# A decoder block on one core: the output product of the next tokens moved in front of the last channel group of the feed-forward part, and GpSimd's tensor operations moved to VectorE

## The chip, the cores and the metric

The kernel runs on one core of a Trainium2 chip. A core has TensorE (PE, matrix products into PSUM), VectorE (DVE), ScalarE (ACT), GpSimd (POOL) and SyncE (SP), which here only issues transfers. Each engine works through its own queue in order. The metric is the device time of one execution in microseconds (us); lower is better. The kernel before took 2862.96 us (median of 3 runs, 2861.45 to 2866.43).

## The reference

One layer of a decoder for 2048 tokens of width 1024, in float32. In outline:

```
h = rmsnorm(x, norm1_g) * (1 + sc1) + sh1
p = h @ w_in                                   # 1024 -> 27 * 128 columns
y = concat(rglru(p...), hgrn2(p...), rwkv7(p...)) * mix_beta
x = x + g1 * (y @ w_out)                       # 1024 -> 1024
h = rmsnorm(x, norm2_g) * (1 + sc2) + sh2
x = x + g2 * ((silu(h @ w_gate) * (h @ w_up)) @ w_down)   # 1024 -> 2816 -> 1024
out = rmsnorm(x, final_g)
```

`sh1, sc1, g1, sh2, sc2, g2` come from the conditioning vector c by one product with `ada_w`. The three mixers are recurrences along the tokens: a gated linear recurrence behind a short convolution, a gated linear attention in chunks, and the delta-rule recurrence of RWKV-7.

## The kernel before

**Layout.** Channels lie on the 128 partitions, tokens along the free dimension. The 2048 tokens are cut into NB = 4 blocks of TB = 512; a tile is 128 channels by 512 tokens, and KC = 8 such tiles make up the width of 1024. D_FF = 2816 gives NF = 22 tiles of the feed-forward part.

**Products.** Every large product goes through `project` (L261). Operands are split in two: `hi`, rounded to the fast float32r format, and `lo`, what is left. A product of one 128x128 weight piece with one tile is three matmuls of 512 columns (`wh*hh`, `wh*hl`, `wl*hh`), L271. The results gather in PSUM banks named `pd`, of which there are 3. Weights come from `load_w` (L250): SyncE loads a tile `wr` (3 buffers), ScalarE makes `wh` and VectorE `wl` (4 buffers each), by `split_v`. The tiles of activations are `hh` and `hl`, 16 buffers each. Float32 tiles of the dense part (inputs, residuals, squares, intermediate results) are all of one name, `xs`, with 12 buffers.

**Order of work.** The program is written as one long list, and a planner sets each engine's queue from it when the kernel is built: it follows the dependencies, hands out the buffers of each name, and prefers the instruction with the smaller priority. The kernel sets the priority by `level(...)`: "out" (adds into the residual) comes first, then "load" (weights), "feed" (the default of the dense part), "mix" (mixers), and "dense" (the matmuls, and the final norm's multiplies) last. The mixers' steps are dealt out between the products by `tick` (L282), by a clock `now` that counts matmul time; `finish(b)` (L294) runs what is left of the mixers up to block b. So mixers overlap with `w_in` and with the feed-forward part of the earlier blocks.

**Stages.** `w_in_products` (L1001) stores the 27 column tiles of p to memory, for blocks 0 and 1, then 2 and 3 (L1111 to L1128); its last five columns run for block 2 and after that for block 3. Then, for each block b:

- `load_y(b)` (L1044): finishes the mixers of b, loads the eight tiles of y (`xs`), and splits them with `split` (L238): ScalarE for `hh`, GpSimd for `hl`.
- `w_out_products(b)` (L1054): for each of 8 channel tiles d the x tile is loaded (`xs`), the product is added to it (it becomes x1[d] and stays), and `square_sum` (L337) squares it into another `xs` tile and adds up. After the first channel it calls `before()`, which is the final norm of block b-1. At its end `rstd_of` (L354) sums over the partitions by matmuls with ones (L363 to L365) and takes Ln and Exp.
- `ffn(b)` (L1084): `make_h` (L388) writes the eight normalized tiles; `ffn_up` makes the 22 tiles g = silu(gate) * up; after each four of them the down products of that group (groups of 4, 4, 4, 4, 4, 2) are added into x1, for the eight channels d. Before the last group stands `load_y(b + 1)`. With the last group the squares for the final norm are taken.

The loop at its heart, with the last group as one of six:

```
for f0 in range(0, NF, 4):
    ...
    if len(gs) == NF and ys is None and b + 1 < NB:
        ys = load_y(b + 1)
    for d in range(KC):
        p, = project(gs[f0:f0 + n], load_w(w_down[d][:, f0 * 128:(f0 + n) * 128], split_v))
        with level("out"):
            stt(x1[d], p, G2[:, d:d + 1], x1[d], OP.mult, OP.add)
```

GpSimd does three things: the `lo` of `load_y` (L240), six additions in the statistics of block 1 (L344), and clearing of tiles (L609).

Of the kernel before, what the change touches and what calls it, by code (L numbers as in the profile page):

```python
# [10 lines left out]
F = mybir.dt.float32  # L11
# [63 lines left out]
def hybrid_kernel(ctx, tc, x, par, ada_w, w_in, rgw, igw, w_up, a_up, g_up, w_out,  # L75
# [14 lines left out]
    @contextmanager  # L90
    def level(name):

        clock[levels[-1]] = tc.cur_priority
        levels.append(name)
        tc.cur_priority = clock[name]
        yield
        clock[name] = tc.cur_priority
        levels.pop()
        tc.cur_priority = clock[levels[-1]]

    def act(o, i, f=AF.Copy, **k):
        return A.activation(o, i, f, **k)

    def stt(o, a, s, b, op0, op1):
        return V.scalar_tensor_tensor(o, a, s, b, op0=op0, op1=op1)
# [38 lines left out]
    def pc(name, i=0):  # L144
        a, b = PCOLS[name]
        assert a + i < b
        return P[:, a + i:a + i + 1]
# [87 lines left out]
                               lambda: bank("pd", 3), xs_)  # L235


    def split(src, hi, lo):  # L238
        act(hi, src)
        G.tensor_sub(lo, src, hi.bitcast(F))  # L240

    def split_v(src, hi, lo):
        i = act(hi, src)
        V.tensor_sub(lo, src, hi.bitcast(F))
        return i
# [4 lines left out]
    def load_w(src, fn):  # L250
        ws = []
        with level("load"):
            for c in range(0, src.shape[1], TB):
                n = min(TB, src.shape[1] - c)
                w = raw_w(src[:, c:c + n])
                hi, lo = w_parts()
                fn(w[:, :n], hi[:, :n], lo[:, :n])
                ws.append((hi, lo))
        return ws

    def project(h, *cols):  # L261

        ps = [bank("pd", 3) for ws in cols]
        tot = 3 * len(h)
        with level("dense"):
            for k, (hh, hl) in enumerate(h):
                c = slice((k % 4) * 128, (k % 4 + 1) * 128)
                for p, ws in zip(ps, cols):
                    wh, wl = ws[k // 4]
                    for n, (a, b) in enumerate(((wh, hh), (wh, hl), (wl, hh)), 3 * k):  # L270
                        PE.matmul(p, a[:, c], b, start=(n == 0), stop=(n == tot - 1))  # L271
                    now[0] += 0.68
                if k % (4 // len(ps)) == 4 // len(ps) - 1 or k == len(h) - 1:
                    tick()
        return ps
# [61 lines left out]
    def square_sum(s, t, k, tile=None, n=1):  # L337

        s, *last = s or (None,)
        if len(last) == n:  # L340
            if s is None:
                s = last.pop(0)
            else:
                (G if tile else V).tensor_add(s, s, last.pop(0))  # L344
        q = (tile or xs_)()
        if k == KC - 1:
            V.tensor_mul(q, t, t)
        else:
            squared[:] = [act(q, t, AF.Square)]
        return s, *last, q  # L350
# [18 lines left out]
    def load_x(src, b, k, tile=None):  # L369
        t = (tile or xs_)()  # L370
        load(t, src[k, :, b * TB:(b + 1) * TB])
        return t
# [15 lines left out]
    def make_h(xt, rs, gain, shift, table=None, ks=range(KC), over=True):  # L388

        hs = []  # L390

        def low(k, t, hi, lo):
            stt(lo, t, shift[:, k:k + 1], hi.bitcast(F), OP.add, OP.subtract)
            hs.append((hi, lo))

        todo = []
        for k in ks:
            x_ = xt(k)
            t = x_ if over else xs_()
            stt(t, x_, gain[:, k:k + 1], rs, OP.mult, OP.mult)  # L400
            hi, lo = parts_()
            i = act(hi, t, AF.Identity, bias=shift[:, k:k + 1])
            todo.append((k, t, hi, lo))
            if len(todo) > 2:
                low(*todo.pop(0))
        for a in todo:
            low(*a)
        if table is not None:
            order(A.preload_act_table_set(table), i)
        return hs  # L410

    def drain(it):
        for _ in it:
            pass
# [586 lines left out]
    def w_in_products(h, cols, side):  # L1001

        n = 0
        while n < len(cols):

            cs_ = cols[n:n + 2] if n == 0 and len(h) == 1 else cols[n:n + 1]
            ws = [W.pop(c) if c in W else load_w(w_in[c], split_v) for c in cs_]
            for i, b in enumerate(h):
                for j, (c, p) in enumerate(zip(cs_, project(h[b], *ws))):
                    with level("feed"):  # L1010
                        t = xs_()
                        if (n + i + j) % 2:
                            act(t, p)
                        else:
                            V.tensor_copy(t, p)
                        SP.dma_start(pd[c, :, b * TB:(b + 1) * TB], t)
                        stored.add((c, b))
                    next(side, None)
            n += len(cs_)
# [24 lines left out]
    def load_y(b):  # L1044
        finish(b)
        ys = []
        for k in range(KC):
            t = load_x(yd, b, k)
            y = parts_()
            split(t, *y)  # L1050
            ys.append(y)
        return ys

    def w_out_products(b, ys, before):  # L1054
        x1, s = [], None
        for d in range(KC):
            ws = load_w(w_out[d], split_v)
            t = load_x(x, b, d)
            p, = project(ys, ws)
            with level("out"):  # L1060
                stt(t, p, G1[:, d:d + 1], t, OP.mult, OP.add)
            if d == 0:
                before()
            s = square_sum(s, t, d)
            x1.append(t)
        return x1, rstd_of(s)

    def ffn_up(h, f):
        if f:
            p, = project(h, load_w(w_gate[f], split_v))  # L1070
        else:
            p, pu = project(h, load_w(w_gate[f], split_v), load_w(w_upf[f], split_v))
        t = xs_()
        with level("out"):
            act(t, p, AF.Silu)
        if f:
            pu, = project(h, load_w(w_upf[f], split_v))
        with level("out"):
            V.tensor_mul(t, pu, t)
        g = parts_()  # L1080
        split_v(t, *g)
        return g

    def ffn(b, x1, rs):  # L1084
        h = make_h(lambda k: x1[k], rs, A2, B2, "silu_and_others", over=False)
        gs, s, ys = [], None, None
        for f0 in range(0, NF, 4):
            n = min(4, NF - f0)
            while len(gs) < min(f0 + n + (2 if f0 + n + 2 >= NF else 1), NF):
                gs.append(ffn_up(h, len(gs)))  # L1090
            if len(gs) == NF and ys is None and b + 1 < NB:
                ys = load_y(b + 1)
            for d in range(KC):
                p, = project(gs[f0:f0 + n], load_w(w_down[d][:, f0 * 128:(f0 + n) * 128], split_v))
                with level("out"):
                    stt(x1[d], p, G2[:, d:d + 1], x1[d], OP.mult, OP.add)
                if f0 + n == NF:
                    s = square_sum(s, x1[d], d, n=1 if b + 1 < NB else 2)

        def final_norm():  # L1100
            rs = rstd_of(s)
            for d in range(KC):
                with level("dense"):
                    stt(x1[d], x1[d], pc("final_g", d), rs, OP.mult, OP.mult)
                    SP.dma_start(out[d, :, b * TB:(b + 1) * TB], x1[d])

        return ys, final_norm

    side = ada_rest()
    NH, NT = 4, 5  # L1110
    for b0 in range(0, NB, 2):  # L1111
        h = {b0: h0}
        if b0 + 1 < NB:
            head, rest = IN_ORDER[:NH], IN_ORDER[NH:-NT]
            w_in_products(h, head, ahead)
            drain(ahead)
            h1 = {b0 + 1: norm1(b0 + 1)}
            w_in_products(h1, head, side)
            h.update(h1)
            ahead = x_stats(range(b0 + 2, min(b0 + 4, NB)), 1)  # L1120
            w_in_products(h, rest, chain(islice(side, 16), ahead, side))
            drain(ahead)
            w_in_products({b0: h[b0]}, IN_ORDER[-NT:], side)
            if b0 + 2 < NB:
                h0 = norm1(b0 + 2)
            w_in_products(h1, IN_ORDER[-NT:], side)
        else:
            w_in_products(h, IN_ORDER, side)  # L1128
    drain(side)
    with level("feed"):  # L1130
        ys, before = load_y(0), lambda: None
    for b in range(NB):
        with level("feed"):
            ys, before = ffn(b, *w_out_products(b, ys, before))
    before()


# [54 lines left out]
```

## Time and profile before

| | |
|---|---|
| time, median of 3 runs | 2862.96 us |
| time of the profiled execution | 2862.48 us |
| its span | 2860.7 us |
| TensorE busy | 2732.2 us (96%) |
| VectorE busy | 1932.6 us (68%) |
| ScalarE busy | 1476.4 us (52%) |
| GpSimd busy | 80.0 us (3%) |
| moved by DMA | 352.27 MB, mean 123 GB/s |
| granted TensorE clock, mean | 0.983 |

The profile is that of one execution. Busy time of TensorE counts overlapping matmuls once. A row of a group has busy time in us, the mean ns of one instruction, and behind the second bar the engine's idle time ahead of these instructions and what ended most of it. A row of the timeline has start and length in us, engine, line, operation, output and inputs, and in brackets the idle time before. L69 is the line of a helper that counts VectorE's and ScalarE's instructions, so those are told apart by their tiles. Most of the kernel's matmuls are those of L271.

### The profile page before, as it was taken

What the parts mean: (1) busy time and instruction counts of PE and PEld (TensorE: products, weight loads), DVE (VectorE), ACT (ScalarE), POOL (GpSimd) and SP (SyncE); (2) the same over time, 40 slices, a digit from 0 to 9 for tenths busy, and PEclk for the clock granted to TensorE, in tenths of its full rate; (3) what the DMA queues carried; (4) which work ended last, traced back from release to release, by engine and by line L of the source; (5) the groups of instructions that cost most, each with busy time, mean ns of one, the idle gap of its engine ahead of it and who ended that gap; (6) DMA issues with size and microseconds to landing.
All of it is one profiled execution on the core that took longest, in us unless ns stands there. A gap on an engine that the chain in (4) does not pass through costs nothing. (4 is left out here: it accounts for less than half of the span.)

```text
span 2860.7 us, 41286 instructions
## 1 busy us (share of the span) xinstructions
PE 2732.2 (96%) x14842; PEld 2196.6 (77%) x14842; DVE 1932.6 (68%) x4112; ACT 1476.4 (52%) x2466; POOL 80.0 (3%) x67
## 2 busy tenths in 40 slices
PE   7999998999998999999989999999999999999998
PEld 6787776777876688877767877877778788788886
DVE  7677667867686875687877858778776445644435
ACT  4433854464547743666477456746773433433333
POOL 2000000000001000001000000010000001000000
PEclk9999999999999999999999999999999999999999
DMA  7553455544444242434333434335233333433332
GB/s 256 186 148 114 137 166 161 160 137 145 128 128 131 93 122 81 141 100 137 108 111 97 122 89 129 113 111 158 75 112 102 93 96 121 145 99 96 97 99 85
DMA packets 242590, 352.27 MB, mean 123 GB/s; under 512 B 72913, under 2 KB 78545, under 8 KB 242385
## 3 DMA queue, kind: packets, MB, share of 16 engines
q1 hardware_dynamic: 160144, 285.55, 31.9%
q10 hardware_dynamic: 82240, 64.09, 8.5%
q8 instruction: 117, 1.92, 0.3%
q14 instruction: 89, 0.72, 0.1%
HBM read 293.92 MB, written 55.62 MB: 122 GB/s over the span
## 5 line engine op out<-in xcount | busy, mean ns | idle before, releaser
L271 PE MATMUL pd<-hh,wh 128*128 128x512 f32 x3232 | 1295.1, 402 | 26.7 <-ACT hh L69 23.2
L271 PE MATMUL pd<-hl,wh 128*128 128x512 f32 x3232 | 1284.6, 398 | 5.0 <-DVE hl L69 3.9
L271 PE MATMUL pd<-hh,wl 128*128 128x512 f32 x3232 | 1282.4, 397 | 1.3 <-DVE wl L69 1.3
L69 ACT ACTIVATE wh<-wr 128x512 fp32r<-128x512 f32 (+1 forms) x752 | 464.0, 620 | 892.8 <-PE pd L271 719.6
L271 PEld LDWEIGHTS pd<-hh,wh 128*128 128x128 f32 x3232 | 613.5, 190 | 154.8 <-ACT hh L69 26.2
L271 PEld LDWEIGHTS pd<-hl,wh 128*128 128x128 f32 x3232 | 613.8, 190 | 136.2 <-DVE hl L69 8.9
L69 DVE TENSOR_TENSOR wl<-wr,wh 128x512 fp32r<-128x512 f32 (+1 forms) x752 | 510.8, 683 | 300.9 <-ACT wh L69 282.0
L271 PEld LDWEIGHTS pd<-hh,wl 128*128 128x128 f32 x3232 | 613.4, 190 | 130.3 <-issue 3.3
L69 ACT ACT_TABLE_LOAD x227 | 291.2, 1283 | 9.1 <-DVE tr L69 2.3
L69 DVE SCALAR_TENSOR_TENSOR xs<-pd,Q,xs 128x512 f32<-128x512 f32 x224 | 167.7, 748 | 141.6 <-PE pd L271 132.8
L69 DVE TENSOR_TENSOR th<-th 128x256 f32<-128x256 f32 (+8 forms) x349 | 155.0, 458 | 29.7 <-ACT th L69 23.3
L69 DVE TENSOR_TENSOR big<-big 128x30 f32<-128x30 f32 (+7 forms) x480 | 117.1, 244 | 10.2
L69 DVE TENSOR_TENSOR xs<-pd,xs 128x512 f32<-128x512 f32 x88 | 60.8, 691 | 87.2 <-PE pd L271 85.3
L69 ACT ACTIVATE xs<-pd 128x512 f32<-128x512 f32 x140 | 82.6, 590 | 69.4 <-PE pd L271 61.5
L69 ACT ACTIVATE th<-th 128x512 f32<-128x512 f32 (+2 forms) x153 | 93.3, 611 | 45.5 <-DVE th L69 25.8
L69 ACT ACTIVATE hh<-xs 128x512 fp32r<-128x512 f32 x120 | 74.4, 628 | 40.4 <-DVE xs L69 24.9
L69 ACT ACTIVATE hw<-big,we 64x64 f32<-64x64 f32 x192 | 66.1, 344 | 46.0 <-DVE big L69 43.1
L69 ACT ACTIVATE tr<-tr 128x512 fp32r<-128x512 f32 (+4 forms) x112 | 69.2, 626 | 13.9 <-DVE tr L69 12.9
L240 POOL TENSOR_TENSOR hl<-xs,hh 128x512 fp32r<-128x512 f32 x32 | 43.2, 1377 | 989.2 <-ACT hh L69 987.5
L69 DVE SCALAR_TENSOR_TENSOR big<-pc,we,hw 64x64 f32<-64x64 f32 x168 | 47.4, 282 | 32.5 <-PE pc L302 28.6
L69 DVE TENSOR_TENSOR tr<-tr 128x512 fp32r<-128x512 f32 (+2 forms) x80 | 54.7, 686 | 18.3 <-ACT tr L69 17.8
L69 DVE TENSOR_TENSOR hl<-xs,hh 128x512 fp32r<-128x512 f32 x88 | 60.7, 689 | 6.2 <-ACT hh L69 2.0
(185 smaller groups left out, 2290.7 us busy)
## 6 DMA issues: line engine op xcount, KB each, us to landing
wr<-in_w_gate SPq DMA_DIRECT2D x176, 256.0 KB, 2.6
wr<-in_w_upf SPq DMA_DIRECT2D x176, 256.0 KB, 2.6
wr<-in_w_down SPq DMA_DIRECT2D x160, 256.0 KB, 2.7
wr<-in_w_in SPq DMA_DIRECT2D x144, 256.0 KB, 3.4
pd<-xs SPq DMA_DIRECT2D x108, 256.0 KB, 3.1
xs<-in_x SPq DMA_DIRECT2D x72, 256.0 KB, 4.2
wr<-in_ada_w SPq DMA_DIRECT2D x64, 256.0 KB, 3.3
th<-pd ACTq DMA_DIRECT2D x64, 256.0 KB, 3.5
```

What stands on the lines that cost most here:

```text
L69: return f(*a, **k)
L240: G.tensor_sub(lo, src, hi.bitcast(F))
L271: PE.matmul(p, a[:, c], b, start=(n == 0), stop=(n == tot - 1))
```

## The change

Two things change.

1. `split` is gone: `load_y` uses `split_v`, whose subtraction runs on VectorE, and the six additions of `square_sum` that ran on GpSimd run on VectorE. GpSimd keeps the clearing of tiles.

2. The order of the dense part. The groups of the feed-forward part are now 2, 4, 4, 4, 4, 4 tiles (`GROUPS`). `ffn` does all of them but the last. With the last but one (for blocks 0 to 2) x1[d] is stored to a buffer in memory, `xr`, and its `xs` tile is given back. Then come `load_y(b + 1)`, `w_out_products(b + 1)` and the normalized tiles of block b+1 (`norm2`), and only then the last group of block b, `ffn_last`: for each d it loads the residual from `xr`, adds the product, stores the result to another buffer, `xf`, and takes the square. The final norm of block b loads `xf` again, tile by tile; it stands in `ffn(b + 1)` after the first three `ffn_up`. Block 3 keeps its x1 in place and uses neither `xr` nor `xf`. For block 0 the output product and `norm2` stand ahead of the last five columns of `w_in` of block 3.

```diff
-    def split(src, hi, lo):
-        act(hi, src)
-        G.tensor_sub(lo, src, hi.bitcast(F))
...
-                (G if tile else V).tensor_add(s, s, last.pop(0))
+                V.tensor_add(s, s, last.pop(0))
...
-            split(t, *y)
+            split_v(t, *y)
...
+    GROUPS = (2, 4, 4, 4, 4, 4)
+
+    def ffn_down(gs, f0, d):
+        p, = project(gs, load_w(w_down[d][:, f0 * 128:(f0 + len(gs)) * 128], split_v))
+        return p
+
+    def norm2(x1, rs):
+        return make_h(lambda k: x1[k], rs, A2, B2, "silu_and_others", over=False)
+
+    def ffn(b, x1, h, before):
+
+        gs, f0 = [], 0
+        for i, n in enumerate(GROUPS[:-1]):
+            while len(gs) < min(f0 + n + 1, NF):
+                gs.append(ffn_up(h, len(gs)))
+            if i == 0:
+                before()
+            if i == len(GROUPS) - 2:
+                while len(gs) < NF:
+                    gs.append(ffn_up(h, len(gs)))
             for d in range(KC):
+                p = ffn_down(gs[f0:f0 + n], f0, d)
                 with level("out"):
                     stt(x1[d], p, G2[:, d:d + 1], x1[d], OP.mult, OP.add)
+                    if b + 1 < NB and i == len(GROUPS) - 2:
+                        SP.dma_start(xr[d, :, b * TB:(b + 1) * TB], x1[d])
+            f0 += n
+        return gs[f0:], f0
+
+    def ffn_last(b, x1, gs, f0):
+        s, ts_ = None, []
+        for d in range(KC):
+            t = load_x(xr, b, d) if b + 1 < NB else x1[d]
+            p = ffn_down(gs, f0, d)
+            with level("out"):
+                stt(t, p, G2[:, d:d + 1], t, OP.mult, OP.add)
+                if b + 1 < NB:
+                    SP.dma_start(xf[d, :, b * TB:(b + 1) * TB], t)
+            s = square_sum(s, t, d, n=1 if b + 1 < NB else 2)
 
         def final_norm():
             rs = rstd_of(s)
             for d in range(KC):
+                with level("feed"):
+                    t = load_x(xf, b, d) if b + 1 < NB else x1[d]
                 with level("dense"):
-                    stt(x1[d], x1[d], pc("final_g", d), rs, OP.mult, OP.mult)
-                    SP.dma_start(out[d, :, b * TB:(b + 1) * TB], x1[d])
-
-        return ys, final_norm
+                    stt(t, t, pc("final_g", d), rs, OP.mult, OP.mult)
+                    SP.dma_start(out[d, :, b * TB:(b + 1) * TB], t)
+
+        return final_norm
...
     with level("feed"):
-        ys, before = load_y(0), lambda: None
-    for b in range(NB):
-        with level("feed"):
-            ys, before = ffn(b, *w_out_products(b, ys, before))
+        x1, rs = w_out_products(0, load_y(0))
+        h = norm2(x1, rs)
+        w_in_products(h1, IN_ORDER[-NT:], side)
+        before = lambda: None
+        for b in range(NB):
+            gs, f0 = ffn(b, x1, h, before)
+            if b + 1 < NB:
+                x1, rs = w_out_products(b + 1, load_y(b + 1))
+                h = norm2(x1, rs)
+            before = ffn_last(b, x1, gs, f0)
     before()
```

More of the change, by code (lines that the diff above doesn't have):

```diff
@@ L1049, in load_y, with w_out_products @@
             y = parts_()
-            split(t, *y)
+            split_v(t, *y)
             ys.append(y)
         return ys
-    def w_out_products(b, ys, before):
+    def w_out_products(b, ys):
         x1, s = [], None
@@ L1061, in w_out_products @@
                 stt(t, p, G1[:, d:d + 1], t, OP.mult, OP.add)
-            if d == 0:
-                before()
             s = square_sum(s, t, d)
@@ L1082, in ffn_up @@
         return g
[L1084 to L1089, printed above, removed]
-                gs.append(ffn_up(h, len(gs)))
-            if len(gs) == NF and ys is None and b + 1 < NB:
-                ys = load_y(b + 1)
+    xr = tc.dram_tile([KC, 128, T], F, name="xr")
+    xf = tc.dram_tile([KC, 128, T], F, name="xf")
+    GROUPS = (2, 4, 4, 4, 4, 4)
[8 more added lines that the diff above has]
+            while len(gs) < min(f0 + n + 1, NF):
+                gs.append(ffn_up(h, len(gs)))
+            if i == 0:
[3 more added lines that the diff above has]
+                    gs.append(ffn_up(h, len(gs)))
             for d in range(KC):
-                p, = project(gs[f0:f0 + n], load_w(w_down[d][:, f0 * 128:(f0 + n) * 128], split_v))
+                p = ffn_down(gs[f0:f0 + n], f0, d)
                 with level("out"):
                     stt(x1[d], p, G2[:, d:d + 1], x1[d], OP.mult, OP.add)
-                if f0 + n == NF:
-                    s = square_sum(s, x1[d], d, n=1 if b + 1 < NB else 2)
+                    if b + 1 < NB and i == len(GROUPS) - 2:
[12 more added lines that the diff above has]
+            s = square_sum(s, t, d, n=1 if b + 1 < NB else 2)
         def final_norm():
@@ L1125, in hybrid_kernel @@
                 h0 = norm1(b0 + 2)
-            w_in_products(h1, IN_ORDER[-NT:], side)
-        else:
-            w_in_products(h, IN_ORDER, side)
+                w_in_products(h1, IN_ORDER[-NT:], side)
     drain(side)
     with level("feed"):
-        ys, before = load_y(0), lambda: None
-    for b in range(NB):
-        with level("feed"):
-            ys, before = ffn(b, *w_out_products(b, ys, before))
+        x1, rs = w_out_products(0, load_y(0))
+        h = norm2(x1, rs)
+        w_in_products(h1, IN_ORDER[-NT:], side)
+        before = lambda: None
[5 more added lines that the diff above has]
+            before = ffn_last(b, x1, gs, f0)
     before()
```

## The prediction

> **What bounds the kernel now.** The page first. Its engine totals say that TensorE is the bound, and its groups say with what.
>
> ```profile
> span 2860.7 us, 41286 instructions
> PE 2732.2 (96%) x14842; PEld 2196.6 (77%) x14842; DVE 1932.6 (68%) x4112; ACT 1476.4 (52%) x2466; POOL 80.0 (3%) x67
> L271 PE MATMUL pd<-hh,wh 128*128 128x512 f32 x3232 | 1295.1, 402 | 26.7 <-ACT hh L69 23.2
> ...
> L240 POOL TENSOR_TENSOR hl<-xs,hh 128x512 fp32r<-128x512 f32 x32 | 43.2, 1377 | 989.2 <-ACT hh L69 987.5
> ...
> L69 DVE TENSOR_TENSOR hl<-xs,hh 128x512 fp32r<-128x512 f32 x88 | 60.7, 689 | 6.2 <-ACT hh L69 2.0
> ...
> wr<-in_w_gate SPq DMA_DIRECT2D x176, 256.0 KB, 2.6
> ...
> xs<-in_x SPq DMA_DIRECT2D x72, 256.0 KB, 4.2
> ```
>
> TensorE is idle for 2860.7 − 2732.2 = 128.5 us, so that is all that hiding stalls can win. The change removes no matmul. Next the busy time by stretches around the transitions between blocks (columns: busy time and instruction count of PE, PEld, DVE, ACT, POOL, then granted clock, DMA share, GB/s).
>
> ```profile
> 858.00:873.00 15.00, 10.41 (x49) 7.77 (x48) 4.43 (x12) 13.26 (x25) 6.55 (x6) 0.89 0.65 206
> 943.00:960.00 17.00, 10.65 (x122) 6.88 (x122) 15.28 (x29) 16.42 (x20) 0.00 (x0) 0.70 0.10 33
> 1350.00:1375.00 25.00, 18.14 (x160) 14.09 (x158) 22.20 (x47) 8.82 (x18) 10.42 (x8) 0.86 0.32 94
> 1463.00:1480.00 17.00, 9.76 (x34) 6.56 (x34) 13.25 (x23) 15.29 (x23) 0.00 (x0) 0.70 0.21 63
> 1898.00:1911.00 13.00, 7.14 (x51) 5.53 (x50) 11.23 (x20) 3.73 (x7) 7.70 (x6) 0.74 0.35 106
> 2000.00:2020.00 20.00, 13.06 (x53) 9.64 (x52) 16.50 (x30) 17.34 (x29) 0.00 (x0) 0.84 0.21 67
> 2473.00:2490.00 17.00, 11.09 (x37) 7.23 (x36) 12.20 (x19) 10.93 (x15) 0.00 (x0) 0.80 0.20 62
> ```
>
> Two kinds of stall stand here. Call the four places where `w_out_products` of block b hands over to its `ffn` T0 to T3 (near 950, 1470, 2010, 2480 us): idle 6.4, 7.2, 6.9 and 5.9 us. The three rows with POOL busy (860, 1360, 1900 us) are `load_y`: idle 4.6, 6.9 and 5.9 us. T3 is the plainest, because no mixer is left there; this is its timeline.
>
> ```profile
> 2477.70 0.75 DVE L69 SCALAR_TENSOR_TENSOR xs<-pd,Q,xs 128x512 f32<-128x512 f32 x1 [0.83 <-PE pd L271]
> 2479.23 1.13 PE L365 MATMUL pd<-xs,aones 128*128 128x512 f32 x2 [1.57 <-DVE xs L69]
> 2482.39 0.63 ACT L69 ACTIVATE rstd<-rstd 128x512 f32<-128x512 f32 x1
> 2484.61 1.22 PE L271 MATMUL pd<-hh,wh 128*128 128x512 f32 x2 [4.26 <-ACT hh L69]
> ...
> L69 DVE SCALAR_TENSOR_TENSOR xs<-xs,Q,rstd x8: 746/747/751, 2483.1 to 2491.0; 128x512 f32<-128x512 f32 x8
> ```
>
> The last product of `w_out` ends just before 2477.7; sum, statistics matmul, Ln, Exp and the first normalized tile take until 2484.6, 6.9 us. After it the matmuls restart slowly:
>
> ```profile
> 2485.00:2491.00 6.00, 5.99 (x20) 4.33 (x20) 6.00 (x10) 3.60 (x6) 0.00 (x0) 0.76 0.00 0
> ...
> 2485.85 353.05 PE pd L271 x1552
> ```
>
> The chain of waits gives 353.05 / 1552 = 0.2275 us for a matmul at full pace, so 6 us should hold 26, not 20: another 1.4 us. T3 costs 6.9 + 1.4 = 8.3 us; I take the same for T0 to T2, 33 us in all, and for `load_y` 17.4 us idle plus about 1.4 each, 21 us. Gains end at about 54 us.
>
> **The order of loads, on which the forecast turns.** The reordered group does not only move matmuls. For blocks 0 to 2 it loads its residual back with `load_x(xr, ...)`, one `xs` tile per channel d, and `square_sum` takes a second. Of 12 `xs` buffers 8 then hold the next block's x1, so 4 rotate. I therefore looked at how such loads run now, in `w_out_products(0)`, whose loop has the same shape. SyncE's queue in order of time, with the squares from the same stretch:
>
> ```profile
> 866.72 0.43 SPq L164 DMA_DIRECT2D xs<-in_x  x1
> 875.75 0.33 SPq L155 DMA_DIRECT2D wr<-in_w_out  x1
> 876.13 0.43 SPq L164 DMA_DIRECT2D xs<-in_x  x1
> 880.50 3.66 SPq L155 DMA_DIRECT2D wr<-in_w_out  x2
> 884.25 0.38 SPq L164 DMA_DIRECT2D xs<-in_x  x1
> 890.58 2.58 SPq L155 DMA_DIRECT2D wr<-in_w_out  x2
> 893.25 0.38 SPq L164 DMA_DIRECT2D xs<-in_x  x1
> ...
> 879.94 0.62 ACT L69 ACTIVATE xs<-xs 128x512 f32<-128x512 f32 x1
> ...
> 889.66 0.61 ACT L69 ACTIVATE xs<-xs 128x512 f32<-128x512 f32 x1
> ...
> DMA to landing us min/median/max: 3.1/3.5/5.9
> ```
>
> By 884 us the y tiles are split, and at most a handful of the 12 buffers are taken; yet the loads of x do not run ahead. They go one per d, each behind two weight loads (a channel of `w_out` has two weight tiles), although nothing they read is late. The reading that fits is that buffers of one name are handed out in program order: the load for d+1 is planned only once the square of d has its buffer. In `w_out` this is harmless: a channel has 24 matmuls, 24 × 0.2275 = 5.5 us, against a landing of 3.5 us. In the moved group a channel has 12, 2.7 us.
>
> **The moved group at T3, step by step.** Time 0 is the last `w_out` matmul.
> - `norm2` stands ahead of the group in program order and takes eight `xs` tiles. Its eighth is written from 2491.0, that is at +13.3; two more weight splits on VectorE (0.69 each, the rate of the same operation in the hl row) make +14.7. Only then is the first residual loaded: +3.5 landing, +0.75 for the add (the row at 2477.70): the first accumulator bank is free at +19.0.
> - TensorE has meanwhile run channels 0 to 2 (`pd` has 3 banks): 3 × 2.7 + 1.1 = 9.3 us. It idles from +9.3 to +19.0.
> - From then on each channel costs add 0.75, issue of the `xf` store 0.33 (as a weight load's), issue of the next load 0.4 (it stands behind that store in SyncE's queue), landing 3.5: 5.0 us, not 2.7.
> - `ffn_up(0)` of the next block needs two banks, the ones freed by adds 5 and 6: 19.0 + 6 × 5.0 = +49.0.
> - The group's own work is 96 × 0.2275 = 21.8 us, which leaves its old place. Net: 49.0 − 21.8 − 8.3 = **+18.9 us**. With a landing of 2.6 us (the page's weight loads) it is 18.1 + 24.5 − 30.1 = +12.5; with 4.2 us (the page's loads of x) 19.7 + 34.1 − 30.1 = +24. If the loads run ahead after all it is −8.3.
>
> **T1 and T2.** First the last store of a mixer, and the stores of the final norm around T1.
>
> ```profile
> 2244.31 0.33 ACTq L69 DMA_DIRECT2D yd<-tr  x1
> ...
> 1414.94 0.34 SPq L1105 DMA_DIRECT2D out<-xs  x1
> ...
> 1444.65 2.63 SPq L1105 DMA_DIRECT2D out<-xs  x4
> ...
> SPq L1105 <- DVE xs L69: 34.3, 24, 15.0
> ```
>
> The same chain, but mixers can use the holes. Their share of TensorE is 2732.2 − 9696 × 0.2275 = 526 us, over about 2244 us (the mixer store), 0.23 us per us. Over 49 us that is 11.5 us of a hole of 49.0 − 21.8 − 1.1 = 26.1; 14.6 us stay idle where 8.3 were lost: +6.3 each, **+13**. Bounds: mixers fill all, −8.3 each; they fill nothing beyond what they do anyway, +18.9 each.
>
> **The final norm** of block b now follows `ffn_up` 0 to 2 of block b+1, and its eight reloaded tiles stand ahead of `ffn_up(3)`'s tile in the same four buffers. Its multiplies have the lowest priority on VectorE: the out stores above show 29 us between one and the next while mixers run. Two rounds of four with one such wait delay `ffn_up(3)` by about 29 + 7; 10.9 us of down products, a gate product of 5.5 and two spare banks, 10.9, hide 27. About 9 us for a starved block; as not each will be, I take 4 each for blocks 0 and 1, **+8** (0 to +40). In exchange the loads of x in `w_out` no longer queue behind these stores, on which SyncE waited 34.3 us; most of that the mixers cover, and I take a tenth, **−3** (0 to −7).
>
> **T0** has no reload: five columns of `w_in` (5 × 5.5 = 27 us) cover the 6.9 us. Their `xs` tiles also come after `norm2`'s, so the third column may wait some 2 us: **−7** (0 to −8.3).
>
> **GpSimd's work on VectorE.** A split's subtraction goes from 1377 to 689 ns, 32 times, and six additions of `x_stats` move too: 38 × 0.69 = 26 us more on VectorE, whose share is 68%. While GpSimd works, VectorE is slowed:
>
> ```profile
> PE pd L271 <- ACT hh L69: 2.9, 1, 2.9
> ...
> 1894.97 0.28 DVE L69 TENSOR_TENSOR big<-big 128x126 f32<-128x126 f32 x1
> 1894.98 9.61 POOL L240 TENSOR_TENSOR hl<-xs,hh 128x512 fp32r<-128x512 f32 x7 [198.78 <-ACT hh L69]
> 1895.60 0.95 DVE L69 TENSOR_TENSOR big<-big 128x126 f32<-128x126 f32 x1
> ```
>
> The first row is the longest wait of a `pd` product near 860 us; in the next three 0.28 becomes 0.95, so a GpSimd operation costs VectorE about as much as doing it. The total is a wash; what improves is that the order written out now knows of the load. Of the 21 us at `load_y` I credit **−8** (0 to −20; the first of the three keeps a wait, since the h of two blocks now fill the 16 `hh` buffers until `w_in`'s last column of block 2).
>
> The 96 added transfers (24 each of `xr`, `xf`, out and back, 256 KB) cost SyncE 96 × 0.4 = 38 us of issue over the second half, where weight loads run up to seven tiles ahead: 0.
>
> [...]
>
> **Sum.** −7 − 8 + 18.9 + 13 + 8 − 3 = +22 us on the profiled execution's 2862.5 us (span 2860.7 plus 1.8 around it), 2884; the median of the runs is 2863.0, 0.5 above it: **2885 us**. Its own range, with every term moved about halfway to its bounds: 2855 to 2920.
>
> **Rivals.**
> - *The loads run ahead.* Then the group covers the chain (21.8 against 6.9 us) everywhere: −33, `load_y` −12, w_out −3, final norms +4: −44, **2819**. For it: the buffers are four and the code order alone asks for no pacing. Against: the queue above, at every d. 0.20.
> - *The loads are paced, but the mixers fill T1 and T2 and the norms are not starved*: +18.9 − 16.6 − 7 − 14 − 3 = −22, **2841**. For it: mixers have two streams ready. Against: they live on VectorE, busy 16.5 of 20 us at T2 already. 0.14.
> - *The stalls only change places* (the change doesn't do what it says): T1, T2 and norms at 0, −7 − 8 + 18.9 − 3 = +1, **2864**. 0.11.
>
> **How the numbers follow.** My forecast has 0.55. 0.2% is 5.7 us, about what a measurement of this kernel can tell. Faster is 0.20 + 0.14 = 0.34, same 0.11, slower 0.55. The range takes in the second and third rival, ends just above the first one's time, where about 0.11 is left below, and cuts the forecast's tail at 2915 with some 0.09 above: 2822 to 2915.
>
> **What would show it.** Right: behind `norm2` at T3, TensorE idles about 10 us after three channels, then in steps of about 5 us with VectorE's add waiting on a transfer into `xs` from `xr`; SyncE alternates `xf` stores and `xr` loads one for one; POOL has no tensor operation, and the `load_y` stretches lose less than 4 us each. Wrong: `xr` loads in a row ahead of the products, TensorE full through T3, and span below 2855.

## The result and the profile after

The changed kernel takes 2892.76 us (median of 4 runs, 2888.9 to 2893.51); the kernel before, beside it, 2862.53 us (median of 4, 2861.45 to 2866.43). The ratio is 1.0101, with a 95% interval of 1.0086 to 1.0116: the change makes the kernel about 1% slower. The profiled execution took 2893.51 us.

The page of the kernel after, with the engine totals and the group of TensorE's first matmul of three:

```profile
span 2891.7 us, 41433 instructions
PE 2737.8 (95%) x14842; PEld 2194.0 (76%) x14842; DVE 1935.4 (67%) x4150; ACT 1502.5 (52%) x2487; POOL 26.5 (1%) x29
...
L267 PE MATMUL pd<-hh,wh 128*128 128x512 f32 x3232 | 1295.4, 401 | 54.5 <-DVE xs L69 45.1
```

The number of matmuls is the same. TensorE idles 2891.7 − 2737.8 = 153.9 us, 25.4 more than before, and is busy 5.6 us longer, at a mean granted clock of 0.981 where it was 0.983. The last row says where the idle time went: ahead of the products it was 26.7 us, mostly for `ACT hh` (the first normalized tile), and is 54.5 us, mostly for `DVE xs`. That is an accumulator bank that the residual's addition has not yet emptied.

Busy time in fixed stretches around T0, T1, T2 and T3, first of the kernel before, then of the one after (columns as in the prediction):

```profile
780.00:1010.00 230.00, 212.66 (x1401) 166.75 (x1400) 174.55 (x411) 149.45 (x258) 14.20 (x12) 0.97 0.38 116
1300.00:1600.00 300.00, 280.80 (x1701) 221.93 (x1700) 236.29 (x512) 197.64 (x329) 14.39 (x12) 0.97 0.40 116
1860.00:2110.00 250.00, 234.25 (x1469) 184.56 (x1469) 196.98 (x440) 161.96 (x284) 12.61 (x10) 0.97 0.39 115
2400.00:2600.00 200.00, 194.09 (x842) 158.36 (x841) 109.05 (x163) 81.14 (x131) 11.50 (x8) 0.98 0.39 119
```

```profile
780.00:1010.00 230.00, 220.31 (x1446) 173.24 (x1446) 183.14 (x425) 151.19 (x262) 3.79 (x4) 0.99 0.40 121
1300.00:1600.00 300.00, 275.49 (x1677) 217.88 (x1676) 222.35 (x493) 195.31 (x324) 3.78 (x4) 0.97 0.47 139
1860.00:2110.00 250.00, 224.71 (x1372) 176.12 (x1371) 185.65 (x424) 152.49 (x265) 1.90 (x2) 0.96 0.48 142
2400.00:2600.00 200.00, 181.93 (x758) 146.29 (x758) 104.94 (x161) 79.88 (x125) 0.00 (x0) 0.95 0.49 152
```

A stretch loses its length less TensorE's busy time, and its length times what the clock lacks to 1. By that count T0 gains 7.6 us of idle time and 230 × 0.02 = 4.6 of clock. T1 loses 5.3, T2 9.5 and 250 × 0.01 = 2.5, T3 12.2 and 200 × 0.03 = 6. Together that is +23.3; the rest of the span's +31 is spread thinly over the other stretches (the largest piece, 2.3 us of idle time, lies between 1010 and 1300 us).

T3 on the timeline of the kernel after:

```profile
2465.89 0.75 DVE L69 SCALAR_TENSOR_TENSOR xs<-pd,Q,xs 128x512 f32<-128x512 f32 x1 [0.86 <-PE pd L267]
...
2481.01 0.74 DVE L69 SCALAR_TENSOR_TENSOR xs<-xs,Q,rstd 128x512 f32<-128x512 f32 x1
2481.12 0.33 SPq L164 DMA_DIRECT2D xs<-xr  x1
2484.01 0.75 DVE L69 SCALAR_TENSOR_TENSOR xs<-pd,Q,xs 128x512 f32<-128x512 f32 x1 [0.27 <-DMA xs<-xr]
2484.79 0.33 SPq L1118 DMA_DIRECT2D xf<-xs  x1
2484.82 0.79 PE L267 MATMUL pd<-hh,wh 128*128 128x512 f32 x1 [9.88 <-DVE xs L69]
2485.17 0.42 SPq L164 DMA_DIRECT2D xs<-xr  x1
2488.59 0.75 DVE L69 SCALAR_TENSOR_TENSOR xs<-pd,Q,xs 128x512 f32<-128x512 f32 x1 [3.83 <-DMA xs<-xr]
2489.36 0.32 SPq L1118 DMA_DIRECT2D xf<-xs  x1
...
2500.08 0.42 SPq L164 DMA_DIRECT2D xs<-xr  x1
2504.17 0.63 ACT L69 ACTIVATE wh<-wr 128x512 fp32r<-128x512 f32 x1 [3.77 <-PE pd L267]
2504.83 0.69 DVE L69 TENSOR_TENSOR wl<-wr,wh 128x512 fp32r<-128x512 f32 x1 [3.70 <-ACT wh L69]
2505.44 0.74 DVE L69 SCALAR_TENSOR_TENSOR xs<-pd,Q,xs 128x512 f32<-128x512 f32 x1
```

The last addition of `w_out` stands at 2465.89, the eighth tile of `norm2` at 2481.01, and the first load of a residual follows it by 0.1 us. The first addition of the group waits for that transfer, and TensorE, three channels in, waits 9.88 us for the addition. Then store and load alternate, one of each per channel.

The last four rows show that the loop changes on its way. The fifth residual is loaded at 2500.08 and has landed 3.0 us later, yet its addition runs only at 2505.44. It stands in VectorE's queue behind a weight split (2504.83). The split has waited 3.70 us for ScalarE's half of it (2504.17), and that 3.77 us for TensorE, which was running a channel's matmuls at half clock (0.50 from 2499.70 to 2503.10). The sixth and seventh addition follow the same pattern, 1.7 and 0.7 us after their residuals have landed.

The longest waits at the other transitions, and at the two later `load_y`, in the same kernel:

```profile
1345.85 1.22 PE L298 MATMUL ph<-th,bones 128*128 128x512 f32 x2 [5.65 <-DVE th L69]
1440.01 0.80 PE L267 MATMUL pd<-hh,wh 128*128 128x512 f32 x1 [11.12 <-DVE xs L69]
1899.06 1.22 PE L298 MATMUL ph<-th,bones 128*128 128x512 f32 x2 [6.17 <-DVE th L69]
1993.24 0.80 PE L267 MATMUL pd<-hh,wh 128*128 128x512 f32 x1 [10.12 <-DVE xs L69]
```

### The profile page after: what moved, and what is told of

The parts are those of the page before. It is cut to its first block, busy times and chain, and to the rows that moved or that the text cites. A ratio compares the mean times of both kernels' runs of the same rounds, so it can differ in the third digit from the quotient of the medians.

```text
span 2891.7 us, 41433 instructions
## 1 busy us (share of the span) xinstructions
PE 2737.8 (95%) x14842; PEld 2194.0 (76%) x14842; DVE 1935.4 (67%) x4150; ACT 1502.5 (52%) x2487; POOL 26.5 (1%) x29
## 5 line engine op out<-in xcount | busy, mean ns | idle before, releaser
L267 PE MATMUL pd<-hh,wh 128*128 128x512 f32 x3232 | 1295.4, 401 | 54.5 <-DVE xs L69 45.1
L69 ACT ACT_TABLE_LOAD x248 | 318.2, 1283 | 17.3 <-DVE pcar L69 4.3
L69 DVE TENSOR_TENSOR th<-th 128x256 f32<-128x256 f32 (+6 forms) x355 | 158.0, 458 | 24.6 <-ACT th L69 19.2
L69 DVE TENSOR_TENSOR big<-big 128x30 f32<-128x30 f32 (+7 forms) x480 | 108.1, 225 | 14.2 <-DMA big<-nd 4.1
L69 DVE TENSOR_TENSOR hl<-xs,hh 128x512 fp32r<-128x512 f32 x120 | 81.8, 688 | 15.2 <-ACT hh L69 11.5
L69 ACT ACTIVATE xs<-xs 128x512 f32<-128x512 f32 x77 | 48.3, 628 | 59.8 <-DVE xs L69 53.9
```

Source lines behind the costliest of these rows:

```text
L69: return f(*a, **k)
```

## The experiments

All times below are medians beside the kernel before on the same chip; that kernel's own median moved between 2857 and 2862 us, so kernels of different groups are compared by their ratios to it. The theory: the residual loads of the last group are late because of what is planned ahead of them, and not because of what they move. The rivals: the added transfers, a mere lack of buffers, and the move of GpSimd's work.

**e1: the move to VectorE alone** (the kernel before, with this part of the change only).

```diff
-            split(t, *y)
+            split_v(t, *y)
...
-                (G if tile else V).tensor_add(s, s, last.pop(0))
+                V.tensor_add(s, s, last.pop(0))
```

> The kernel before with GpSimd's tensor operations on VectorE, and nothing else of the change. Theory (the order of the residual loads makes the loss): worth nothing either way, 2858 to 2867 us, since TensorE's progress in the first 800 us was the same in both kernels and the stalls at the gated outputs' loads stayed. Rival, the move itself costs (VectorE is fuller): 2870 us or more. My prediction's own step (a gain of 8 us): 2855 us.

Measured: 2846.69 us, ratio 0.9948 (0.9934 to 0.9961). The theory's number was wrong: the move by itself gains 15 us. T1 and T2 of e1:

```profile
1300.00:1600.00 300.00, 290.22 (x1749) 230.02 (x1748) 241.23 (x530) 200.14 (x335) 3.79 (x4) 0.99 0.41 119
1860.00:2110.00 250.00, 237.52 (x1493) 187.12 (x1491) 203.92 (x459) 159.00 (x283) 1.90 (x2) 0.99 0.40 117
```

Idle time falls from 19.2 to 9.8 us in the first and from 15.8 to 12.5 in the second, and the clock rises from 0.97 to 0.99 in both. In the old order the waits at `load_y` do shrink: the longest are 2.07 and 1.64 us, where they were 4.60 and 5.86. The loss of the change therefore lies wholly in its other part, and is larger than the +30 us that the result shows: 1.0101 / 0.9948 = 1.0154, or 44 us.

VectorE's busy time in e1 is 1934.4 us against 1932.6, with 38 operations more, so the prediction's wash holds for the sum. What is gone at `load_y` is GpSimd's work (busy 3.79 and 1.90 us in the two stretches, where it was 14.39 and 12.61), beside which an operation of VectorE took 0.95 us in the prediction's rows, where 0.28 was usual; and TensorE's longest waits there, the 4.60 and 5.86 us, were for VectorE. That the 15 us come from this is argued and not tested by itself.

**e2: the new order alone** (the changed kernel, the subtraction and the six additions on GpSimd again; the diff of e1 the other way round).

> The changed kernel, but with GpSimd's tensor operations back on GpSimd. Theory: the whole loss is in the new order, so the time is that of the changed kernel, 2887 to 2899 us. Rival, the move to VectorE is the loss: 2865 us or less.

Measured: 2898.94 us, ratio 1.0130 (1.0115 to 1.0144). The loss is there without the move. In the new order the move is worth 1.0130 − 1.0101, about 8 us, and not 15; the two intervals overlap by 0.0001, so the 8 us are barely clear of noise. T1 to T3 idle as in the changed kernel (23.9, 24.8 and 17.4 us); T0 does not:

```profile
780.00:1010.00 230.00, 215.35 (x1418) 168.96 (x1417) 174.17 (x413) 147.81 (x261) 14.26 (x12) 0.99 0.39 118
```

14.7 us idle here, 9.7 with the move: 5.0 of the 8 us lie there.

**e3: the squares out of the way of the loads.** The squares of the last group take buffers of `hl` in blocks 0 to 2, so no residual load has a square's buffer ahead of it.

```diff
+    def q_():
+        return dp.tile([128, TB], R, name="hl", bufs=16).bitcast(F)
...
-            s = square_sum(s, t, d, n=1 if b + 1 < NB else 2)
+            s = square_sum(s, t, d, q_ if b + 1 < NB else None, n=1 if b + 1 < NB else 2)
```

> The changed kernel, with the squares of the last channel group (blocks 0 to 2) in buffers of hl, so that no residual load from xr stands behind a square; norm2's eight tiles stay ahead of the loads. Theory: the holes of 10 us after three channels stay at all three transitions, the later steps of 5.0 to 6.6 us fall to 2.7 to 3.3 us at T3; some 9 us at T3, 1 to 2 us at T1 and T2: 2882 us (2876 to 2888). Rival, the added 25 MB of transfers or SyncE's issue sets the steps: they stay at 5 to 6.6 us and the time at 2893 us.

Measured: 2880.48 us, ratio 1.0071 (1.0054 to 1.0088). The holes stay (11.03, 10.47 and 9.93 us), and the steps behind them go: the eight additions at T3 stand between 2483.37 and 2500.00 us, 2.4 us apart, where the changed kernel has them 5.7 us apart (2484.01 to 2523.76). Idle time in the T3 stretch falls from 18.1 to 10.3 us. The traffic is the same, so the later steps came from the place that the squares' buffers gave the loads in the plan.

**e4: `norm2` out of the way too.** As e3, and `norm2`'s eight temporary tiles in buffers of `hl`.

```diff
-            t = x_ if over else xs_()
+            t = x_ if over else dp.tile([128, TB], F, name="hl", bufs=16)
```

> As the run before, and norm2's eight temporary tiles in buffers of hl too, so that nothing of norm2 stands ahead of the residual loads. The traffic is that of the changed kernel. Theory: the holes of 10 us go as well, the three transitions lose at most 2 us each: 2893.5 less 18.9 (T3), 11.1 (T1), 11.6 (T2) = 2852 us (2840 to 2860), faster than the kernel before. Rival, added transfers: 2880 us or more. Rival, stalls only change places (the gated outputs' rows or norm2's own tiles are late next): 2862 to 2875 us.

Measured: 2862.20 us, ratio 0.9996 (0.9982 to 1.0010). 30 us of the loss is gone with the same transfers, but the number is that of the rival for which stalls only change places, and so is the timeline of e4 at T3:

```profile
2470.29 0.74 DVE L69 SCALAR_TENSOR_TENSOR xs<-pd,Q,xs 128x512 f32<-128x512 f32 x1
...
2480.75 2.19 ACT L69 ACTIVATE hl<-xs 128x512 f32<-128x512 f32 x4
2481.40 1.88 SPq L164 DMA_DIRECT2D xs<-xr  x4
...
2485.56 0.76 PE L267 MATMUL pd<-hh,wh 128*128 128x512 f32 x1 [7.23 <-DVE xs L69]
```

The execution shown took 2870.09 us, the longest of the ten. The first four residuals now load from 2457.95 on, ahead of `norm2`, and the first four additions run by 2471. Then the squares, whose `hl` buffers stand behind those of `norm2`, wait until 2480.75; the next four loads (2481.40) wait for the squares, and TensorE waits 7.23 us.

**e5: the new order at T0 alone**, on top of e1. Blocks 1 to 3 go in the order of before.

```diff
...
-        ys, before = load_y(0), lambda: None
-    for b in range(NB):
-        with level("feed"):
+        x1, rs = w_out_products(0, load_y(0), lambda: None)
+        h = norm2(x1, rs)
+        w_in_products(h1, IN_ORDER[-NT:], side)
+        ys, before = ffn(0, x1, rs, h)
+        for b in range(1, NB):
             ys, before = ffn(b, *w_out_products(b, ys, before))
```

> The kernel before with GpSimd's tensor operations on VectorE (as in e1, 2846.7 us) and with the change's order at T0 alone: block 0's output product and norm2's tiles ahead of the five last input products; blocks 1 to 3 in the order of before. Theory (T0 is the part of the new order that gains, by the stalls of 2.94 and 3.29 us that norm2 leaves there in e1; T1 to T3 are its loss): 2840 us (2836 to 2844). Rival, what T0 gains comes back at T1, where the mixers then have less work left to fill with: 2845 to 2850 us.

Measured: 2839.18 us, ratio 0.9934 (0.9922 to 0.9946): faster than both kernels, and the lowest ratio of the study. Against e1 it is 0.0014, 4 us, with intervals that overlap, so a gain over e1 is not shown. Its T0 stretch idles 10.3 us at a clock of 1.00, against 13.8 at 0.96 in e1; but e1's profiled execution (2850.43 us) lies 4 us above its median.

**e6: the gated outputs earlier.** The changed kernel with `load_y(b + 1)` ahead of the fifth group's eight products.

```diff
...
+                ys = load_y(b + 1) if b + 1 < NB else None
             for d in range(KC):
                 p = ffn_down(gs[f0:f0 + n], f0, d)
...
-                x1, rs = w_out_products(b + 1, load_y(b + 1))
+                x1, rs = w_out_products(b + 1, ys)
```

> The changed kernel, with the gated outputs of the next block loaded and split ahead of the fifth group's eight products instead of behind them; everything else as changed. Theory (a second loss of the new order: the mixers' rest and the gated outputs now end with no product left to cover them, 5.65 and 6.17 us): both stalls fall to about 2 us, 2885 us (2881 to 2889). Rival, the stalls stay since the mixers' rest is as long wherever it is asked for: 2893 us.

Measured: 2891.79 us, ratio 1.0122 (1.0105 to 1.0139): no difference from the changed kernel, and the two waits stay, 4.54 and 6.63 us. The rival held. What shortens these waits in e1 is not the place of the call; the study doesn't settle what it is.

**e7: each load ahead of the square before it**, same buffers.

```diff
-        s, ts_ = None, []
+        s, ts_ = None, [load_x(xr, b, 0)] if b + 1 < NB else []
...
-            t = load_x(xr, b, d) if b + 1 < NB else x1[d]
+            t = ts_.pop(0) if b + 1 < NB else x1[d]
...
+            if b + 1 < NB and d + 1 < KC:
+                ts_.append(load_x(xr, b, d + 1))
             s = square_sum(s, t, d, n=1 if b + 1 < NB else 2)
```

> The changed kernel with the same buffers, but the load of channel d+1's residual is planned ahead of the square of channel d; norm2's tiles stay ahead of the first load. Theory (program order sets the pace): first holes of 10 to 11 us stay, later steps at T3 fall from 5.75 to some 3 to 4 us: 2885 us (2880 to 2889). Rival, four rotating buffers are too few whatever the order: 2890 to 2896 us, steps as before.

Measured: 2898.02 us, ratio 1.0141 (1.0127 to 1.0155). Neither number holds. At T3 it does what the theory says: additions every 3.0 us (2500.34 to 2521.10), idle time 11.9 instead of 18.1 us. T1 to T3 of e7:

```profile
1300.00:1600.00 300.00, 273.93 (x1646) 215.52 (x1644) 216.44 (x483) 185.62 (x313) 3.79 (x4) 0.95 0.47 137
1860.00:2110.00 250.00, 225.16 (x1258) 177.82 (x1256) 191.43 (x421) 152.01 (x258) 0.00 (x0) 0.94 0.48 144
2400.00:2600.00 200.00, 188.15 (x814) 153.24 (x813) 109.36 (x168) 83.73 (x131) 0.00 (x0) 0.97 0.51 162
```

T3 gains 6.2 us of idle time and 4 of clock. T1 and T2 lose 1.6 and gain 0.5 us of idle time, and both run 0.02 slower in clock, 11 us together. There the mixers seem to have filled the steps between channels anyway. So order alone shortens the steps, as the theory had it, but only T3 shows a gain from that. Why the clock falls at T1 and T2 is open, and so is most of the 11 us by which e7 is slower than the changed kernel (1.0141 against 1.0101): the three stretches together account for some 2 us.

**e8: the transfers alone.** The kernel before with 48 stores of residuals and 48 copies within memory, on SyncE's queue; nothing reads the copies.

```diff
...
+                    if b + 1 < NB and f0 == 16:
+                        SP.dma_start(xr[d, :, c], x1[d])
+                    if b + 1 < NB and f0 == 20:
+                        SP.dma_start(xf[d, :, c], x1[d])
+                        SP.dma_start(xq[d, :, c], xr[d, :, c])
...
+                if b + 1 < NB:
+                    SP.dma_start(xg[d, :, c], xf[d, :, c])
```

> The kernel before with the change's transfers alone: 24 stores of the residual after the fifth group, 24 after the last, and 48 copies of 256 KB within device memory where the change loads them back; nothing waits for them. Theory (the added traffic costs nothing): 2858 to 2866 us. Rival, the traffic and SyncE's issue take part of the loss: 2870 us or more.

Measured: 2896.66 us, ratio 1.0134 (1.0114 to 1.0154). The theory's number fell: 38 us, as much as the new order loses without the move (e2, 37 us). TensorE idles 147.6 us, 19.1 more than before, and is busy 16.7 us longer with as many matmuls, at a mean granted clock of 0.979 where it was 0.983, so nearly half of the loss is matmuls that take longer. In the T3 stretch e8 idles 15.9 us. What the SyncE queue waited for between 2425 and 2530 us in e8 (us in total, times, longest), and rows of its timeline:

```profile
SPq L1104 <- DMA xr<-xs: 12.7, 6, 3.5
```

```profile
2452.24 0.42 ACT L69 ACTIVATE wh<-wr 128x256 fp32r<-128x256 f32 x1 [4.89 <-DMA wr<-in_w_down]
...
2453.92 0.76 PE L271 MATMUL pd<-hh,wh 128*128 128x512 f32 x1 [4.22 <-DVE xs L69]
```

The copies wait in SyncE's queue for the stores, 12.7 us in all, and the loads of `w_down` stand behind them; the weights come late in the one group with two tiles, whose channels take 6 × 0.2275 = 1.4 us. So transfers can be as dear as that where weight loads queue behind them. It doesn't say that they are so in the changed kernel, whose last group has four tiles; e12 keeps its 96 transfers and takes what e1 takes, which has none of them.

**e9: `norm2`'s tiles in `hl`, squares back in `xs`** (the changed kernel with the one line of e4 only).

> The changed kernel with norm2's eight temporary tiles in buffers of hl; the squares stay in xs, and each residual load still stands behind the square of the channel before. Theory (what stands ahead of the first load makes the holes of 10 to 11 us, and in e4 the fourth channel waited only because the squares had been put behind norm2's tiles): no hole over 4 us at T1 to T3, TensorE's idle time at T3 below 12 us; 2893 less 31 us of holes, with some 3 us of later steps back: 2862 us (2852 to 2872). Rival, the hole only moves (norm2's tiles or the gated outputs late next), as in e4: holes of 6 us or more stay, 2875 to 2890 us.

Measured: 2869.98 us, ratio 1.0044 (1.0029 to 1.0058), within the theory's range. No wait over 3.6 us is left at T1 to T3 (3.30, 3.50, 3.58), and T3 idles 8.7 us; the steps stay at 4.6 to 7.2 us. At `load_y` 4.61 and 3.34 us remain.

**e10: e9 with e7's order of loads.**

> As e9, and the load of channel d+1 planned ahead of the square of channel d: nothing but a buffer's own user stands ahead of a load. Theory: the best that this order gives with these buffers: no hole over 3 us at T1 to T3, steps of 2.7 to 3.3 us, 2852 us (2842 to 2860), above the 2839 us of e5, since VectorE has norm2's 16 passes, the adds, the square sums and the weight splits in the same stretch. Rival, the added transfers set the pace there: 2870 us or more.

Measured: 2872.99 us, ratio 1.0047 (1.0032 to 1.0061). The time is the rival's, the reason isn't. Holes of 6.00, 5.18 and 8.37 us are back, the first two ahead of mixers' products and the third ahead of the group's own; e10 at T3:

```profile
2473.75 0.32 SPq L164 DMA_DIRECT2D xs<-xr  x1
...
2484.96 1.40 DVE L69 SCALAR_TENSOR_TENSOR hl<-hl,Q,hh 128x512 fp32r<-128x512 f32 x2
2486.28 0.68 DVE L69 TENSOR_TENSOR xs<-xs 128x512 f32<-128x512 f32 x1
2486.99 0.63 ACT L69 ACTIVATE xs<-xs 128x512 f32<-128x512 f32 x1 [1.17 <-DVE xs L69]
2487.65 1.72 SPq L164 DMA_DIRECT2D xs<-xr  x2
```

The fourth load is issued at 2473.75, the fifth only at 2487.65: it waits for a square (2486.99), which waits for a sum of squares (2486.28), which VectorE does only after the last of `norm2`'s passes (2484.96). Here no buffer of `norm2` is in the way. Its instructions are: same priority, earlier in the list.

**e11: the 48 added stores made twice**, in the changed kernel.

```diff
...
                         SP.dma_start(xr[d, :, b * TB:(b + 1) * TB], x1[d])
+                        SP.dma_start(xs2[d, :, b * TB:(b + 1) * TB], x1[d])
...
                     SP.dma_start(xf[d, :, b * TB:(b + 1) * TB], t)
+                    SP.dma_start(xf2[d, :, b * TB:(b + 1) * TB], t)
```

> The changed kernel with each of its 48 added stores made a second time, to a place that nobody reads: 12.6 MB and 48 issues on SyncE's queue more. Theory (the stalls come from buffers, the traffic is covered): 2890 to 2898 us. Rival, the added transfers are a loss of their own, as e8 hints: 2903 us or more.

Measured: 2903.00 us, ratio 1.0158 (1.0143 to 1.0174), clear of the changed kernel's 1.0101: 16 us. The theory's number fell here too. The T3 stretch of e11:

```profile
2400.00:2600.00 200.00, 178.23 (x742) 142.89 (x742) 102.78 (x157) 78.23 (x122) 0.00 (x0) 0.94 0.57 175
```

21.8 us idle instead of 18.1, and T1 and T2 grow by 3.1 and 3.5 us. From a store to the next load SyncE's queue takes about 0.4 us (2484.79 to 2485.17 in the kernel after); a second store there comes ahead of the load too, and the eight additions stand 6.2 us apart instead of 5.7. Where the addition waits for its load, another store per channel is on the path.

**e12: the sums ahead of `norm2`.** As e10, and the squares and their sums in the last group get the priority of the residual's additions.

```diff
-            s = square_sum(s, t, d, n=1 if b + 1 < NB else 2)
+            with level("out" if b + 1 < NB else "feed"):
+                s = square_sum(s, t, d, n=1 if b + 1 < NB else 2)
```

> As e10, and the squares and their sums in the last channel group planned with the residual's additions, ahead of norm2's passes. In e10 the fourth and later residual loads stood behind norm2's 16 passes on VectorE by way of the square sums (hole of 8.4 us at T3). Theory of VectorE's share (16 x 0.74 of norm2 and 8 x 2.12 of additions, weight splits and square sums are 28.8 us, where the eight channels of the group are 22 us of TensorE's work): the hole goes, and TensorE waits some 5 to 8 us for norm2's first or later tiles at the next block's up products instead: 2866 to 2876 us. Rival, place in the queue is all: no wait over 2 us from the last output product to the second up product at T3, 2848 to 2862 us.

Measured: 2846.34 us, ratio 0.9953 (0.9936 to 0.9970). The rival held in its waits, and the time is 1.7 us below its range: the place in the queue was what was left. T1 to T3 of e12, and what is left at T3:

```profile
1300.00:1600.00 300.00, 285.17 (x1689) 225.25 (x1688) 223.97 (x494) 187.00 (x318) 3.79 (x4) 0.98 0.48 143
1860.00:2110.00 250.00, 238.79 (x1352) 189.00 (x1351) 194.70 (x422) 149.55 (x253) 0.00 (x0) 0.99 0.51 152
2400.00:2600.00 200.00, 196.50 (x855) 159.46 (x854) 105.83 (x162) 81.21 (x127) 0.00 (x0) 1.00 0.46 144
```

```profile
2465.81 0.47 PE L267 MATMUL pd<-hh,wh 128*128 128x512 f32 x1 [1.73 <-DVE xs L69]
...
2474.70 0.50 PE L267 MATMUL pd<-hl,wh 128*128 128x512 f32 x1 [1.02 <-DVE hl L69]
```

T3 idles 3.5 us at full clock, less than before the change, and `norm2`, now last in VectorE's queue, costs the next block's product 1.02 us. My sum of VectorE's work (28.8 us against 22 of TensorE's) left out that the next block's first gate and up products use the normalized tiles one by one, over 48 × 0.2275 = 10.9 us; so there was room. From e10 to e12 it is one level: 0.0094, or 27 us. Against the changed kernel it is 42 us, with the same matmuls and the same 96 transfers.

Still, e12 only equals e1, which has none of the new order, and e5 lies 0.0019 below it. At T1 e12 idles 14.8 us, e5 8.8. So nothing here shows a gain from the last three transitions, which need the 96 transfers. The first may be worth some 4 us, which is not settled.

## Why the prediction was right, and where not

**The time.** 2885 us was forecast and 2892.8 measured; the mechanism was the one named. The sum of terms was +22, the measured change +30. Several terms are off in both directions, as below, so that the total comes so near is partly luck.

**T3, +18.9.** By the stretches it is 12.2 + 6 = 18.2. Step by step from the last matmul of `w_out` (just before 2465.89): first load at +14.7 in the prediction, +15.3 in the trace; first bank free at +19.0, and 2484.01 + 0.75 gives +18.9; TensorE idle 9.7 against 9.88. The steps were put at 5.0 us and are 5.7 on average. The first three are 4.6, 4.6 and 5.8, and wait for transfers; the next three are 6.5, and there it is the weight split on VectorE, behind matmuls at half clock (0.50 and 0.51 in the rows of the last section), that the addition waits for (the last rows of the T3 timeline). The prediction's steps had neither. The size came out nonetheless for two reasons that it didn't have: the next block's gate product started with one free bank at 2512.89, +47.0, where the prediction waited for a second bank until +49.0 (it comes free with the seventh addition, 2518.54 + 0.75, at +53.4); and a third of the 18.2 us is clock, where the 18.9 were nearly all waiting.

**T1 and T2, +13.** They lost 5.3 + 9.5 + 2.5 = 17.3. The mixers filled less of the first hole than their mean share: the waits are 11.12 and 10.12 us, as long as T3's 9.88. They seem to have filled the later steps instead: in e7 shorter steps bring nothing at T1.

**The reason.** "Buffers of one name are handed out in program order" was right as far as it went: e3 removes the steps by giving the squares other buffers, e9 the first hole by giving `norm2`'s tiles others. It was not the whole. e10 has no buffer of `norm2` ahead of a load and waits 8.37 us all the same, because the sums of squares stand behind `norm2`'s 16 passes in VectorE's own queue. The prediction named who waits for a buffer, not who waits behind the instruction on the same engine; that step was incomplete. In the changed kernel the same omission shows in the later additions at T3, behind a weight split; it cost the number little, as the first cause mostly hid the second.

**T0, −7.** The order alone (e2 against the kernel before) gives 17.3 − 14.7 = 2.6 us of idle time and 230 × 0.02 = 4.6 of clock, 7.2 in that stretch. In whole times, e5 against e1, it is 4 us with overlapping intervals: the stretch agrees with the sign, and the whole times settle neither sign nor size.

**GpSimd's work on VectorE, −8.** In the changed kernel about 8 us, as put, with intervals that touch; but the place was wrong. The waits at `load_y`, which were to fall below 4 us, stayed at 5.65 and 6.17; the gain sits at T0. And the term wasn't the same in both orders: 15 us in the old one (e1). The prediction called the total a wash and looked only at the waits.

**The final norms, +8.** Too much. After the hole at T1 there is no wait over 1.4 us until 1899 us; `ffn_up(3)` was not starved; nor is there one over 1.5 us between T2's hole and T3, or over 0.7 us in the 180 us behind T3's. The 8 us that did not come nearly equal the 7.7 us lost outside the four stretches, for which no cause was found: that is luck. No run sets apart the −3 for the loads of x in `w_out`.

**The added transfers, 0.** Wrong as a rule, since e11 pays 16 us for 48 stores more. The issue time on SyncE was counted against free time over half the kernel, but half of the stores sit in the loop that is paced. Where the loop isn't paced the term may be 0: e12 carries all 96 and takes what e1 takes.

**The rivals.** "The loads run ahead" is e12, and the price was wrong: 2846 us, not 2819. With the loads early, T1 still idles 14.8 us and T2 11.2. The longest waits left there are 3.85 us at `load_y` and 1.88 us in the mixers' products, and not those of the chain that the group was to cover.

## What to carry to other kernels

Before work is moved ahead of other work, list for each load in the moved part what is planned ahead of it: the buffers of its name, and then, for the instruction that frees its buffer, what stands ahead of that one in its engine's queue. The second half was worth 27 us here by one level of priority, and was mostly hidden by the first. And split a change: of its two parts one gained 15 us alone and the other lost 37 us alone, and with the other at one place of four the kernel takes 2839 us, against 2893 for the whole.

## What the hardware showed

TensorE's clock at T3, in stretches of 3.4 us of the kernel after:

```profile
2492.90:2496.30 3.40, 2.25 (x10) 1.91 (x11) 2.04 (x3) 0.88 (x2) 0.00 (x0) 1.00 0.48 161
2496.30:2499.70 3.40, 0.72 (x4) 0.26 (x2) 1.44 (x2) 0.63 (x1) 0.00 (x0) 1.00 0.55 145
2499.70:2503.10 3.40, 3.27 (x8) 2.63 (x9) 0.69 (x1) 0.63 (x1) 0.00 (x0) 0.50 0.60 204
2503.10:2506.50 3.40, 1.43 (x7) 0.90 (x6) 1.35 (x2) 0.85 (x2) 0.00 (x0) 0.99 0.00 0
2506.50:2509.90 3.40, 3.40 (x9) 2.61 (x9) 0.69 (x1) 0.41 (x1) 0.00 (x0) 0.51 0.71 231
2509.90:2513.30 3.40, 1.44 (x6) 0.89 (x6) 1.35 (x2) 1.09 (x2) 0.00 (x0) 0.99 0.06 8
2513.30:2516.70 3.40, 3.40 (x10) 2.66 (x9) 0.69 (x1) 0.17 (x1) 0.00 (x0) 0.51 0.67 223
```

In these rows the granted clock is 0.99 to 1.00 or 0.50 to 0.51. The two stretches that were 42% busy (1.43 and 1.44 of 3.40) and the one that was 21% busy (0.72) are each followed by one at half clock; the one that was 66% busy (2.25) is followed by one at 1.00. Two of the waits:

```profile
2494.05 0.47 PE L267 MATMUL pd<-hh,wh 128*128 128x512 f32 x1 [1.34 <-DVE xs L69]
...
2506.33 0.58 PE L267 MATMUL pd<-hh,wh 128*128 128x512 f32 x1 [1.97 <-DVE xs L69]
```

Behind the wait of 1.34 us the clock stayed at 1.00, behind the one of 1.97 it was 0.51. In e9 the matmuls stood 0.43 us apart, as they do here at half clock, from 1.5 us after a wait of 1.81 us (2482.54 to 2484.67), and 0.23 us apart behind the next wait, of 1.77 us (from 2487.38 on); so the lengths of the waits lie close together, and what decides is not shown. In the loop, three products in a row have a half-clock stretch (first matmuls at 2499.83, 2506.33 and 2512.89), and each is followed by the next after some 6.5 us, nearly two of these stretches.
